# A gated hybrid decoder layer in split fp32: a sixth set of block products, block sums spread over two products, linear attention's sums on VectorE, channel tiles ahead of the branch products

## Chip, cores and metric

One core of one Trainium2 chip. The metric is the device time of one execution in microseconds (us): the median of several runs. Besides, one execution was profiled.

## What is computed

One layer (`DEPTH` = 1) on 256 tokens of 2048 channels. A normalised input goes through one wide projection; two causal mixers run in parallel (gated linear attention with 4 heads, differential attention with 16 heads); each result is gated and projected, the two are merged by sigmoid gates, projected once more and added to the input.

```python
h = rmsnorm(x, pre_norm_g)
a_q, a_k, a_v, a_g, a_lr, b_q, b_k, b_v, b_g, m_a, m_b = split(h @ w_in)
gk  = log_sigmoid(a_lr @ gla_gk_w2 + gla_gk_b) / 16
o_a = gla_chunked(a_q, a_k, a_v, gk)                # S_t = diag(exp(gk_t)) S_{t-1} + k_t^T v_t ; o_t = q_t S_t
y_a = (rmsnorm(o_a) * silu(a_g)) @ w_branch_a
o_b = diff_attention(b_q, b_k, b_v, lam)            # (softmax(q1 k1) - lam * softmax(q2 k2)) v, 128 wide per head
y_b = (rmsnorm(o_b) * (1 - lam_init) * silu(b_g)) @ w_branch_b
out = (sigmoid(m_a) * y_a + sigmoid(m_b) * y_b) @ w_out
x   = x + rmsnorm(out, post_norm_g)
```

All in fp32.

## The kernel before

**Split weights.** Every weight tile is split into a high part (a rounded copy by ScalarE, L244) and a low part (the rest, by VectorE, L245), and the activations likewise. A product is three passes on TensorE: high x high, low x high, high x low. The weights come in "halves" of 128 x 1024 elements, in the order of the list `seq` (L158 to L161). `take` (L252) hands the next half to the matmuls, and `emit_half` (L228) loads and splits up to `AHEAD` = 4 halves before it is used; high and low parts have three buffers each.

**Three ways to use a half.** `token_major` (L424) makes a 512-wide key in two banks: eight halves, twelve 128x512 matmuls each. `channel_major` (L446) makes one 128-wide channel tile (`dq`, `dk`) from two halves, with equal TensorE work per half. The third is `block_products` (L672): two 512-wide keys are made together, as a 2x2 block matrix product with seven products in place of eight (`PRODUCTS`, L28, in the order 1, 3, 5, 6, 2, 7, 4). Each product takes four halves ("half-steps") of six 128x512 matmuls. Its weight operands are blocks and sums of blocks, kept in two chains `a` and `b` (two tiles `t` of two halves `h` each): `a` is loaded, used by product 1, gets block 2 added by an accumulating DMA from the POOL queue, is used by product 5, gets `b` added on VectorE (L192) for product 6, and so on. The set's sums on VectorE are L192 (at product 6) and L199 (at product 2, with the block in `raws`). Products 1, 6, 7 and 4 add up in one PSUM bank `x`; L717 and L724 read it in between.

**Stages.** First `v0`, `v2`, `v3` directly. Then the set stage: `phase_steps` (L77) mixes the sets' half-steps with 64 "other" halves (`v4`, the linear attention's `k` and `q`, group 0's channel tiles, `m00`) by `other[len(other) * i // len(steps) : ...]` after half-step `i`. With `SETS` = 5, set 0 and 1 are merge gates and set s (s over 1) makes `dv` and `bg` (values and gates of attention group s - 2); group 3's `dv3` and `bg3` are made directly in `diff_heads(3)`. Set results are spilled to DRAM and fetched when needed. Then `ag0` to `ag3`, `m01`, attention groups 0 and 1 (`diff_heads`, L988), `m02`, the linear branch's products `y00` to `y03`, groups 2 and 3, `m03`, the attention branch's `y10` to `y13`, and the output projection `o0` to `o3`.

**Tasks.** The attention work is written as generators in a list `tasks`. `pump(step)` (L381) advances the first `step` tasks to their next `yield`; `token_major` calls it after every second half, `diff_heads` after every channel tile. Tasks in order: `forget_gate`, two `gla_scores` (one for each half of the linear heads), two `gla_out`, and for each group two `diff_pair` (two heads each; group g waits for both pairs of group g - 1). `settle` (L1059), called within `y10`, advances whatever is left until the list is empty. The order of instructions on each engine is then fixed at build time by a scheduler that starts from this order; buffers come from pools: `u` 18 tiles of 4 KB (`BIG`), `u2` 13 (`MORE`), and four PSUM banks each with the tags `mm` and `bg`. The tag `u2` holds, among others, the linear branch's operands `oah`, `oal` (four each, until `y03` is done) and the attention branch's `obh`, `obl` (one each per group, until `y13`).

**Group tiles.** For groups in `STORED` the channel tiles `dq`, `dk` are spilled and fetched by `diff_pair`; for the others `diff_split` runs at once.

Of the kernel before, what the change touches and what calls it, by code (L numbers as in the profile page):

```python
# [25 lines left out]
ROWS = {"two": 2, "tok": 4, "chan": KT}  # L26
WARM = 8
PRODUCTS = (1, 3, 5, 6, 2, 7, 4)  # L28
SETS = 5
LEAD = 6  # L30
EARLY = (0,)
STORED = (0, 1, 2)
BIG = 18
MORE = 13
BRIDGE = 512
# [56 lines left out]
def hybrid_kernel(ctx: ExitStack, tc, xt, xn, preg, postg, w, w2, gkb, glag, lamv, diffg, ident_d, causal_d, lmask_d, out):  # L92
# [57 lines left out]
    def halves_of(*keys):  # L150
        return [(key, r, h) for key in keys for r in range(len(at[key])) for h in range(2)]

    def heads_order(g):
        values = (f"dv{g}", f"bg{g}") if g + 2 >= SETS else ()
        chans = [] if g in EARLY else [f"{name}{g}{c}" for pair in range(2) for name in ("dq", "dk") for c in (2 * pair, 2 * pair + 1)]
        return halves_of(*values, *chans)

    seq = halves_of("v0", "v2", "v3") + phase_steps()  # L158
    seq += halves_of(*(f"ag{g}" for g in range(4)), "m01") + heads_order(0) + heads_order(1) + halves_of("m02")
    seq += halves_of(*(f"y0{g}" for g in range(4))) + heads_order(2) + heads_order(3) + halves_of("m03")  # L160
    seq += halves_of(*(f"{name}{g}" for name in ("y1", "o") for g in range(4)))  # L161
    ready = {}
    emitted = [0]
    raws = {}
    chain = {}

    def weights(key, r):
        a, size = at[key][r]
        return w[a : a + P * size].rearrange("(p n) -> p n", p=P), size
# [7 lines left out]
    def emit_set(s, prod, t, h):  # L177
        c = slice(1024 * h, 1024 * h + 1024)
        if h == 0 and prod == 1:
            if s == 0:  # L180
                link(s, "a", t)
            link(s, "b", t)
        if h == 0 and prod == 4 and s + 1 < SETS:
            link(s + 1, "a", t)
        n = 4 * PRODUCTS.index(prod) + 2 * t + h + LEAD - 4 * PRODUCTS.index(2)
        if 0 <= n < 4:
            i, j = n // 2, n % 2
            raws[s, i, j] = u([P, 1024], "c")
            sp.dma_start(raws[s, i, j], weights(f"set{s}", 4 + i)[0][:, 1024 * j : 1024 * j + 1024])
        a, b = chain[s, "a", t], chain[s, "b", t]  # L190
        if prod == 6:
            dve.tensor_tensor(out=a[:, c], in0=a[:, c], in1=b[:, c], op=ALU.add)  # L192
        return raws[s, t, h] if prod == 2 else (b if prod in (3, 7) else a)[:, c]

    def follow_set(s, prod, t, h):
        c = slice(1024 * h, 1024 * h + 1024)
        a, b = chain[s, "a", t], chain[s, "b", t]
        if prod == 2:
            dve.tensor_tensor(out=a[:, c], in0=a[:, c], in1=raws[s, t, h], op=ALU.add)  # L199
        if h == 1 and prod in (1, 6):  # L200
            pool.dma_start(a if prod == 1 else b, weights(f"set{s}", 2 + t)[0], accum_op=ALU.add)

    def emit_plain(j, key, r, h):
        src, size = weights(key, r)
# [47 lines left out]
    def take(key):  # L252
        j = used[0]
        used[0] += 1
        while emitted[0] < min(j + 1 + AHEAD, len(seq)):
            emit_half()
        e, hi, lo = ready.pop(j)
        assert key in (e, e[0]), (e, key)
        return hi, lo
# [118 lines left out]
    done = set()  # L378
    latest = [None]

    def pump(n=1):  # L381
        with tc.issue_after(latest[0]):
            for task in tasks[:n]:
                if next(task, DONE) is DONE:
                    tasks.remove(task)

    def product(out, pairs, first, last):
        for n, (lhs, rhs) in enumerate(pairs):
# [35 lines left out]
    def token_major(key, n, ops, step=1, settle=None):  # L424
        banks = [ps("mm"), ps("mm")]
        for q in range(KT // 2):
            if q == 6 and settle:
                settle()
            half_tile(banks, n, q, ops, *take(key))
            if q % 2 or "gate" not in done:  # L430
                pump(step)
        return banks

    def half_channel(o, h, hi, lo):
        turns = [(w, j) for w in (hi, lo) for j in range(8)]
        if h:
            turns.append(turns.pop(7))
        for w, j in turns:
            kt, c = 8 * h + j, slice(P * j, P * j + P)
            if w is hi:  # L440
                i = pe.matmul(o, hi[:, c], x_pair(kt), start=kt == 0, stop=kt == KT - 1)  # L441
            else:
                i = pe.matmul(o[:, :S], lo[:, c], x_ops(kt)[0], start=False, stop=False)  # L443
        latest[0] = i.ins

    def channel_major(key):  # L446
        o = ps("mm")
        for h in range(2):
            half_channel(o, h, *take(key))
        return o[:, :S], o[:, S:]  # L450

    def gate(bank, b, dst):
# [297 lines left out]
    def gla_scores(hf):  # L750
# [13 lines left out]
        def add_pairs(dst, src, n):  # L764
            dst = dst.rearrange("p (g t) -> p g t", t=n)
            src = src.rearrange(pairs, i=2, t=n)
            pool.tensor_tensor(out=dst, in0=src[:, :, 0, :], in1=src[:, :, 1, :], op=ALU.add)

        pool.tensor_tensor(out=suf, in0=q, in1=k, op=ALU.mult)
        add_pairs(es[:, :512], suf.rearrange("p b c t -> p (b c t)"), P)  # L770
        pool.memset(suf, 0.0)
        yield
        for n, m in enumerate(LEVELS):
# [8 lines left out]
            act.activation(xqv, view(pre, m, *late), AF.Exp, scale=1.0 / 16.0)  # L782
            dve.tensor_tensor(out=xqv, in0=xqv, in1=view(q, m, *late), op=ALU.mult)
            if m == 1:
                pool.tensor_tensor(out=xqv, in0=xqv, in1=view(k, 0, *early), op=ALU.mult)
                add_pairs(es[:, 512:], xq, 64)
                act.activation(eh, es, AF.Copy)
                dve.tensor_tensor(out=el, in0=es, in1=f32(eh), op=ALU.subtract)
                pool.memset(a, 0.0)
            else:  # L790
                act.activation(xkv, view(suf, 0, *early), AF.Exp, scale=1.0 / 16.0)
                dve.tensor_tensor(out=xkv, in0=xkv, in1=view(k, 0, *early), op=ALU.mult)
# [34 lines left out]
        act.activation(ah, aall, AF.Copy)  # L827
        dve.tensor_tensor(out=al, in0=aall, in1=f32(ah), op=ALU.subtract)
        done.add(f"scores{hf}")
        yield  # L830

    for hf in range(2):
        tasks.append(gla_scores(hf))
# [4 lines left out]
    def gla_out(hf, gates):  # L838
# [27 lines left out]
        for j in range(4):  # L866
            bank = ps("bg")
            for h in range(2):
                for b in range(2):
                    pe.transpose(bank[:, P * (2 * h + b) : P * (2 * h + b) + P], og[h][:, b, P * j : P * j + P], ident)  # L870
            i = 2 * hf + j // 2
            hi = oah[i][:, j % 2].rearrange("p h t -> p (h t)")
            lo = oal[i][:, j % 2].rearrange("p h t -> p (h t)")
            split_out(bank, hi, lo, glag_s[:, j : j + 1])
            if j % 2:
                yield
        done.add(f"out{hf}")

# [28 lines left out]
    def diff_pair(g, pair, values):  # L907
# [15 lines left out]
        for h in (2 * pair, 2 * pair + 1):  # L923
# [50 lines left out]
            dve.tensor_tensor(out=e, in0=e, in1=half_rstd, op=ALU.mult)  # L974
            for b in range(2):
                dve.scalar_tensor_tensor(out=og[:, h % 2, b, :], in0=bank[:, P * b : P * b + P], scalar=e[:, b : b + 1], in1=uu[:, b, hv], op0=ALU.mult, op1=ALU.mult)
            yield
        bank = ps("bg")
        for i in range(2):
            for b in range(2):  # L980
# [2 lines left out]
        lo = ol[:, 2 * pair : 2 * pair + 2, :].rearrange("p h t -> p (h t)")  # L983
        split_out(bank, hi, lo, diffg_s)
        done.add(f"pair{g}{pair}")
        yield

    def diff_heads(g):  # L988
        values = []
# [35 lines left out]
        return obh[kt // 4][:, kt % 4, :], obl[kt // 4][:, kt % 4, :]  # L1025

    merge_gate(token_major("m01", 512, x_ops, 2))
    diff_heads(0)
    diff_heads(1)
    merge_gate(token_major("m02", 512, x_ops, 2))  # L1030

    while not {"out0", "out1"} <= done:
        pump()
    half_done = []
    for g in range(4):
# [7 lines left out]
                act.activation(t, banks[b], AF.Copy)  # L1043
        if g < 3:
            half_done.append(spill(part, "part"))

    diff_heads(2)
    diff_heads(3)

    banks = token_major("m03", 512, x_ops, 2)  # L1050
    for b in range(2):
# [166 lines left out]
```

## Time and profile before

| | |
|---|---|
| median of 3 runs | 1121.78 us (1121.51 to 1122.82) |
| profiled execution | 1123.6 us, span from first to last instruction 1121.8 us |
| granted TensorE clock, mean | 0.997 |
| busy: PE / PEld / DVE / ACT / POOL | 1105.6 / 945.4 / 831.8 / 677.1 / 111.8 us |
| HBM read, written | 236.86 MB, 19.92 MB |

PE is TensorE's matmuls, PEld its weight loads, DVE VectorE, ACT ScalarE, POOL GpSimd, SP the queue that issues most loads. A row of a group reads: line, engine, operation, output <- inputs, shape, count, busy us, mean ns of one, and the idle time of that engine just before, with what ended most of it. A timeline row has start, duration, engine, line, and in brackets the idle time before it. A row by stage has the stretch, its length, the busy time and number of instructions of each engine, the clock, the DMA engines' share and GB/s.

### The profile page before, as it was taken

The page shows a single profiled execution, that of the slowest core. Times are in us where ns is not written, and L with a number is a line of the kernel's source. Part 1 is how long each engine was busy: PE and PEld are TensorE (multiplying, and loading weights), DVE is VectorE, ACT ScalarE, POOL GpSimd, SP SyncE. Part 2 cuts the span into 40 slices and gives each one's busy share as a digit, 9 for nine tenths or more (in the row PEclk, how much of TensorE's full clock was granted, in tenths as well). Part 3 has the DMA queues.
Part 4 walks back from the last instruction along what each step waited for, and adds up shares of the span by engine and source line. Part 5 has one row for each costly group of instructions (what it writes and reads, how often), then busy time and mean ns, then how long its engine had stood idle before and what let it go on. Part 6 is the DMA issues. An engine that isn't in the chain of part 4 may idle for free. (4 is left out here: it accounts for less than half of the span.)

```text
span 1121.8 us, 15070 instructions
## 1 busy us (share of the span) xinstructions
PE 1105.6 (99%) x5570; PEld 945.4 (84%) x5570; DVE 831.8 (74%) x1160; ACT 677.1 (60%) x997; POOL 111.8 (10%) x165
## 2 busy tenths in 40 slices
PE   9999999999999999999999999999999999999996
PEld 7998888888888888878888888788888888788886
DVE  7878979779789798699965866766676766655463
ACT  7856666666666666765655755655675665444450
POOL 0101010000100100340021202111200010000000
PEclk9999999999999999999999999999999999999998
DMA  8799797696996973945586567565645474556752
GB/s 313 261 412 243 260 321 221 221 304 188 336 254 218 313 210 123 317 167 185 174 291 243 200 220 257 202 228 176 237 165 184 158 308 161 180 188 218 269 188 75
DMA packets 46042, 257.76 MB, mean 230 GB/s; under 512 B 5841, under 2 KB 7377, under 8 KB 23441
## 3 DMA queue, kind: packets, MB, share of 16 engines
q1 hardware_dynamic: 31968, 198.59, 49.4%
q0 software_dynamic: 12992, 56.89, 18.1%
q10 hardware_dynamic: 1008, 1.32, 0.4%
q8 instruction: 43, 0.70, 0.2%
q14 instruction: 31, 0.25, 0.1%
HBM read 236.86 MB, written 19.92 MB: 229 GB/s over the span
## 5 line engine op out<-in xcount | busy, mean ns | idle before, releaser
L245 DVE TENSOR_TENSOR lo<-raw,hi 128x1024 fp32r<-128x1024 f32 (+3 forms) x307 | 369.1, 1205 | 183.8 <-ACT hi L244 180.8
L244 ACT ACTIVATE hi<-raw 128x1024 fp32r<-128x1024 f32 (+3 forms) x307 | 315.8, 1032 | 282.0 <-PE mm L421 144.6
L421 PE MATMUL mm<-hi,xs 128*128 128x512 f32 (+1 forms) x704 | 171.4, 385 | 0.0
L421 PEld LDWEIGHTS mm<-hi,xs 128*128 128x128 f32 x704 | 130.2, 188 | 21.2
L245 DVE TENSOR_TENSOR lo<-a,hi 128x1024 fp32r<-128x1024 f32 x80 | 97.2, 1221 | 19.0 <-ACT hi L244 18.0
L244 ACT ACTIVATE hi<-a 128x1024 fp32r<-128x1024 f32 x80 | 84.7, 1059 | 39.4 <-PE mm L706 20.0
L441 PE MATMUL mm<-xs,hi 128*128 128x512 f32 x384 | 100.5, 396 | 0.0
L441 PE MATMUL bg<-xs,hi 128*128 128x512 f32 x384 | 99.5, 390 | 0.2 <-ACT hi L244 0.2
L421 PE MATMUL mm<-lo,xs 128*128 128x512 f32 (+1 forms) x352 | 91.9, 383 | 0.7 <-DVE lo L245 0.7
L441 PEld LDWEIGHTS bg<-xs,hi 128*128 128x128 f32 x384 | 72.1, 188 | 14.7 <-ACT hi L244 0.6
L441 PEld LDWEIGHTS mm<-xs,hi 128*128 128x128 f32 x384 | 69.2, 189 | 11.8
L421 PEld LDWEIGHTS mm<-lo,xs 128*128 128x128 f32 x352 | 65.8, 188 | 12.9 <-DVE lo L245 1.6
L706 PE MATMUL mm<-hi,xs 128*128 128x512 f32 x240 | 65.1, 393 | 0.8 <-DVE gr L724 0.8
L443 PEld LDWEIGHTS bg<-xs,lo 128*128 128x128 f32 x384 | 52.3, 190 | 4.9 <-DVE lo L245 1.2
L443 PEld LDWEIGHTS mm<-xs,lo 128*128 128x128 f32 x384 | 52.4, 190 | 3.8
L245 DVE TENSOR_TENSOR lo<-b,hi 128x1024 fp32r<-128x1024 f32 x40 | 48.6, 1221 | 8.5 <-ACT hi L244 7.8
L443 PE MATMUL bg<-xs,lo 128*128 128x256 f32 x384 | 53.6, 282 | 0.8 <-DVE lo L245 0.8
L443 PE MATMUL mm<-xs,lo 128*128 128x256 f32 x384 | 53.5, 282 | 0.0
L706 PEld LDWEIGHTS mm<-hi,xs 128*128 128x128 f32 x240 | 44.4, 188 | 9.7 <-DVE gr L724 1.5
L421 PE MATMUL mm<-hi,oah 128*128 128x512 f32 x128 | 50.7, 396 | 0.0
L421 PE MATMUL mm<-hi,obh 128*128 128x512 f32 x128 | 50.7, 399 | 0.0
L421 PE MATMUL mm<-hi,obl 128*128 128x512 f32 x128 | 50.1, 392 | 0.0
(301 smaller groups left out, 1966.6 us busy)
## 6 DMA issues: line engine op xcount, KB each, us to landing
raw<-in_w_dram SPq DMA_DIRECT2D x136, 1024.0 KB, 5.0
raw<-in_w_dram SPq DMA_DIRECT2D x14, 832.0 KB, 6.0
a<-in_w_dram SPq DMA_DIRECT2D x10, 1024.0 KB, 6.3
b<-in_w_dram SPq DMA_DIRECT2D x10, 1024.0 KB, 7.4
c<-in_w_dram SPq DMA_DIRECT2D x20, 512.0 KB, 10.3
a<-in_w_dram POOLq DMA_DIRECT2D x10, 1024.0 KB, 15.1
b<-in_w_dram POOLq DMA_DIRECT2D x10, 1024.0 KB, 9.5
raw<-in_w_dram SPq DMA_DIRECT2D x4, 800.0 KB, 9.7
```

Source lines behind the costliest of these rows:

```text
L244: act.activation(hi_t[:, a:b], r[:, a:b], AF.Copy)
L245: dve.tensor_tensor(out=lo_t[:, a:b], in0=r[:, a:b], in1=f32(hi_t[:, a:b]), op=ALU.subtract)
L421: i = pe.matmul(banks[b][:, :n], a[part][:, P * b : P * b + P], w[:, n * j : n * j + n], start=first, stop=last)
L441: i = pe.matmul(o, hi[:, c], x_pair(kt), start=kt == 0, stop=kt == KT - 1)
L443: i = pe.matmul(o[:, :S], lo[:, c], x_ops(kt)[0], start=False, stop=False)
L706: i = pe.matmul(out, a[part], w[:, 512 * j : 512 * j + 512], start=first, stop=last, skip_group_check=out is x)
```

## The change

`SETS` becomes 6, so `dv3` and `bg3` are a sixth set, mixed with the same 64 other halves. The eight sums of a set move: `a` tile 0 gets `b` tile 0 added after the second tile of product 5, tile 1 after the first tile of product 6, and likewise for the sum at product 2 (after the second tile of 2 and the first of 7); the DMA that accumulates into `b` follows each sum of the first kind. Four elementwise operations of each `gla_scores` go from POOL to VectorE. Group 3's channel tiles are spilled and fetched too. Groups 2 and 3 are made ahead of `y00` to `y03`, with `m02` between them. `pump_eager` steps, at halves at which no `pump` is called, those of the first two tasks that stand after a pair's first head. Some `yield`s at the end of tasks go. `settle` is called after the first half of `y10`, not after the sixth.

```diff
-SETS = 5
+SETS = 6
-STORED = (0, 1, 2)
+STORED = (0, 1, 2, 3)
...
     seq = halves_of("v0", "v2", "v3") + phase_steps()
-    seq += halves_of(*(f"ag{g}" for g in range(4)), "m01") + heads_order(0) + heads_order(1) + halves_of("m02")
-    seq += halves_of(*(f"y0{g}" for g in range(4))) + heads_order(2) + heads_order(3) + halves_of("m03")
+    seq += halves_of(*(f"ag{g}" for g in range(4)), "m01") + heads_order(0) + heads_order(1) + heads_order(2)
+    seq += halves_of("m02") + heads_order(3) + halves_of(*(f"y0{g}" for g in range(4)), "m03")
...
         a, b = chain[s, "a", t], chain[s, "b", t]
-        if prod == 6:
-            dve.tensor_tensor(out=a[:, c], in0=a[:, c], in1=b[:, c], op=ALU.add)
         return raws[s, t, h] if prod == 2 else (b if prod in (3, 7) else a)[:, c]
 
     def follow_set(s, prod, t, h):
         c = slice(1024 * h, 1024 * h + 1024)
-        a, b = chain[s, "a", t], chain[s, "b", t]
-        if prod == 2:
-            dve.tensor_tensor(out=a[:, c], in0=a[:, c], in1=raws[s, t, h], op=ALU.add)
-        if h == 1 and prod in (1, 6):
-            pool.dma_start(a if prod == 1 else b, weights(f"set{s}", 2 + t)[0], accum_op=ALU.add)
+
+        def accumulate(name, i):
+            pool.dma_start(chain[s, name, i], weights(f"set{s}", 2 + i)[0], accum_op=ALU.add)
+
+        if prod == 1 and h == 1:
+            accumulate("a", t)
+        i = {(5, 1): 0, (6, 0): 1, (2, 1): 0, (7, 0): 1}.get((prod, t))
+        if i is not None:
+            a = chain[s, "a", i][:, c]
+            second = prod in (5, 6)
+            dve.tensor_tensor(out=a, in0=a, in1=chain[s, "b", i][:, c] if second else raws[s, i, h], op=ALU.add)
+            if second and h == 1:
+                accumulate("b", i)
...
+    eager = set()
+
+    def advance(some):
+        with tc.issue_after(latest[0]):
+            for task in some:
+                r = next(task, DONE)
+                (eager.add if r == "go" else eager.discard)(task)
+                if r is DONE:
+                    tasks.remove(task)
+
     def pump(n=1):
-        with tc.issue_after(latest[0]):
-            for task in tasks[:n]:
-                if next(task, DONE) is DONE:
-                    tasks.remove(task)
+        advance(tasks[:n])
+
+    def pump_eager():
+        advance([task for task in tasks[:2] if task in eager])
...
-            if q == 6 and settle:
+            if q == 1 and settle:
                 settle()
             half_tile(banks, n, q, ops, *take(key))
             if q % 2 or "gate" not in done:
                 pump(step)
+            else:
+                pump_eager()
...
             half_channel(o, h, *take(key))
+            if h == 0:
+                pump_eager()
...
-            pool.tensor_tensor(out=dst, in0=src[:, :, 0, :], in1=src[:, :, 1, :], op=ALU.add)
-
-        pool.tensor_tensor(out=suf, in0=q, in1=k, op=ALU.mult)
+            dve.tensor_tensor(out=dst, in0=src[:, :, 0, :], in1=src[:, :, 1, :], op=ALU.add)
+
+        dve.tensor_tensor(out=suf, in0=q, in1=k, op=ALU.mult)
...
-                pool.tensor_tensor(out=xqv, in0=xqv, in1=view(k, 0, *early), op=ALU.mult)
+                dve.tensor_tensor(out=xqv, in0=xqv, in1=view(k, 0, *early), op=ALU.mult)
...
         done.add(f"scores{hf}")
-        yield
...
-            if j % 2:
+            if j == 1:
                 yield
         done.add(f"out{hf}")
...
-            yield
+            yield "go" if h % 2 == 0 else None
...
         done.add(f"pair{g}{pair}")
-        yield
...
-    diff_heads(0)
-    diff_heads(1)
+    for g in range(3):
+        diff_heads(g)
     merge_gate(token_major("m02", 512, x_ops, 2))
+    diff_heads(3)
...
-
-    diff_heads(2)
-    diff_heads(3)
```

## The prediction, made before the change was run

> **What bounds the kernel now.** I read the page first, then busy time by stage, then what TensorE waited for, then the groups by line.
>
> ```profile
> PE 1105.6 (99%) x5570; PEld 945.4 (84%) x5570; DVE 831.8 (74%) x1160; ACT 677.1 (60%) x997; POOL 111.8 (10%) x165
> ...
> PEclk9999999999999999999999999999999999999998
> ```
>
> TensorE is busy for 99% of the span at the full granted clock, so the order of its instructions is the time. The other engines matter only where TensorE stands still for them. The stages (columns: PE, PEld, DVE, ACT, POOL busy, clock, DMA share, GB/s):
>
> ```profile
> 80.70:447.00 366.30, 364.38 (x1794) 309.30 (x1793) 311.70 (x311) 237.26 (x265) 29.20 (x41) 1.00 0.80 248
> 447.00:500.00 53.00, 52.45 (x236) 42.78 (x234) 39.27 (x32) 38.30 (x51) 24.67 (x24) 1.00 0.69 241
> 500.00:592.00 92.00, 91.75 (x484) 78.74 (x484) 79.09 (x109) 50.84 (x70) 5.89 (x11) 1.00 0.66 228
> ...
> 640.00:755.00 115.00, 114.09 (x561) 95.86 (x560) 76.96 (x162) 67.98 (x130) 12.88 (x23) 1.00 0.64 224
> ...
> 946.70:958.20 11.50, 10.67 (x53) 8.16 (x52) 6.89 (x22) 6.42 (x16) 0.69 (x1) 1.00 0.44 167
> ...
> PE bg L981 <- DVE ogb L976: 1.5, 2, 0.9
> PE bg L443 <- DVE lo L245: 0.8, 1, 0.8
> PE mm L706 <- DVE gr L724: 0.8, 2, 0.5
> PE mm L421 <- DVE lo L245: 0.7, 2, 0.5
> ```
>
> The first row is the stage of the block products ("set stage"), then the forget gate, the linear attention's scores, the branch products y0, and the point in y1 where the last attention tasks are flushed. TensorE stands still for 1.92, 0.55, 0.25, 0.91 and 0.83 us in them, 4.46 us in all. That is everything a better order can bring. Nearly every wait is for VectorE (DVE), which in the set stage works 311.7 of 366.3 us (85%).
>
> **Part 1: the sixth set.** The price of a 128x512 matmul comes from the chain of waits, where TensorE runs without a break:
>
> ```profile
> 972.68 16.35 PE mm L421 x72
> ```
>
> That is 0.227 us each. Direct, `dv3` and `bg3` take 2 keys x 8 halves x 12 = 192 of these matmuls. As a set they take 7 products x 4 halves x 6 = 168. So 24 go: **-5.44 us**, all on the path. What the set adds beside TensorE:
>
> ```profile
> L245 DVE TENSOR_TENSOR lo<-a,hi 128x1024 fp32r<-128x1024 f32 x80 | 97.2, 1221 | 19.0 <-ACT hi L244 18.0
> L244 ACT ACTIVATE hi<-a 128x1024 fp32r<-128x1024 f32 x80 | 84.7, 1059 | 39.4 <-PE mm L706 20.0 <-PE bg L441 10.2 <-PE mm L421 3.8
> ...
> L192 DVE TENSOR_TENSOR a<-a,b 128x1024 f32<-128x1024 f32 x20 | 24.3, 1221 | 0.2
> ...
> L684 DVE SCALAR_TENSOR_TENSOR gr<-tanh,gr 128x512 f32<-128x512 f32 x6 | 4.1, 685 | 0.0
> L724 DVE TENSOR_TENSOR gr<-mm,p 128x512 f32<-128x512 f32 x5 | 3.4, 685 | 0.0
> ```
>
> On DVE: 28 splits and 8 block sums at 1.22 us, 4 sums of products (L714, L717, L721, L724, one form) and 2 gate operations (L684) at 0.685 us, 48.0 us. TensorE gets 168 x 0.227 = 38.1 us more in this stage. DVE then has 359.7 us of work in 404.4 us: 89% in place of 85%. It stays below TensorE, with 44.7 us of slack in place of 54.6, over six sets. ScalarE's 28 x 1.06 us fit its 65% easily. The 16 direct halves leave the later stage, where DVE had room. Two tiles more are spilled and fetched (512 KB each), and the set reads 10 MB where the direct keys read 8; the stage moves 248 GB/s, its DMA share 0.80, and one set adds in proportion to its time. I cost this at nothing; if the DMA engines were the cover that is gone, it shows as the accumulate below.
>
> **Part 2: sums spread over two products.** The number and price of the sums stay (8 per set). Now all eight sit in products 6 and 2, eight half-steps in a row, in each of which DVE has 2.44 us of work against 1.36 us of TensorE. The change puts four at products 5/6 and four at 2/7, with four free half-steps between, so DVE can catch up once. Against it stands the thinner mixing: 64 other halves (2.73 us of TensorE and only 1.22 of DVE each) lie between 168 half-steps, not 140. The row of L724 shows a second spot: product 4 accumulates into the bank that L724 must read first. By the mixing formula an other half fills that spot in two of five sets now, in two of six then. Today the stage idles 1.92 us, 0.38 a set. I take 0.45 a set, 2.7 us: **+0.8**, between -1.9 (none left) and +3 (the 0.5 and 0.8 us waits above once per unfilled spot and set).
>
> **Part 3: the accumulating transfer.** In each set, `a` is read by product 1, then POOL issues a DMA that adds block 2 to it, and product 5 reads it. Issue, what ScalarE (ACT) waited, and TensorE's start (first matmul of the second half of product 5), for set 0:
>
> ```profile
> 86.08 0.89 POOL L201 DMA_DIRECT2D a<-in_w_dram  x1 [0.85 <-DVE vl L531]
> ...
> 101.69 1.06 ACT L244 ACTIVATE hi<-a 128x1024 fp32r<-128x1024 f32 x1 [2.48 <-DMA a<-in_w_dram]
> ...
> 103.35 0.40 PE L706 MATMUL mm<-hi,r1h 128*128 128x512 f32 x1
> ...
> 151.90 0.90 POOL L201 DMA_DIRECT2D a<-in_w_dram  x1
> ...
> 171.38 0.39 PE L706 MATMUL mm<-hi,r1h 128*128 128x512 f32 x1
> ...
> a<-in_w_dram POOLq DMA_DIRECT2D x10, 1024.0 KB, 15.1
> b<-in_w_dram POOLq DMA_DIRECT2D x10, 1024.0 KB, 9.5
> ...
> DMA to landing us min/median/max: 8.0/11.2/18.0
> ```
>
> In set 0 the use follows the issue by 17.3 us; the landing takes 15.1 in the median and up to 18.0, and the split must run about 1.4 us before TensorE can begin (1.06 for the high part and 1.22 for the low, which is wanted four matmuls later, 0.91). The margin is thin, and the page's shares do not show it. Seven half-steps lie between issue and use. In set 1 (last two timeline rows, first half of product 5) three other halves lie among them: 7 x 1.36 + 3 x 2.73 = 17.7 us, against 171.38 - 151.90 = 19.5 measured, so the issue leads TensorE by 1.8. Counting the formula's places, three or four other halves lie there in every set now. After the change only two do in four of the twelve transfers: 9.5 + 5.5 + 1.8 = 16.8 us, enough for a landing at 15.1, not for 18.0. I take 0.3 us for each of the four: **+1.2**, between 0 and 4 x 2.6 = 10.4 (all four at 18.0 + 1.4). The `b` accumulates are issued earlier than now (after 5/6, not 6) and need 9.5 us: nothing. [...]
>
> **Part 4: linear attention's sums on VectorE.** Per half of the heads four POOL operations move:
>
> ```profile
> 463.61 2.46 POOL L769 TENSOR_TENSOR suf<-q,k 128x1024 f32<-128x1024 f32 x1 [6.57 <-DMA k<-k]
> ...
> L767 POOL TENSOR_TENSOR att<-suf 128x512 f32<-128x512 f32 x2 | 4.0, 1980 | 0.1
> L785 POOL TENSOR_TENSOR xq<-xq,k 128x512 f32<-128x512 f32 x2 | 3.3, 1628 | 15.5 <-DVE xq L783 15.5
> ...
> 483.43 0.70 DVE L783 TENSOR_TENSOR xq<-xq,q 128x512 f32<-128x512 f32 x1 [0.21 <-ACT xq L782]
> ...
> 487.66 2.90 DVE L783 TENSOR_TENSOR xq<-xq,q 128x512 f32<-128x512 f32 x1
> 490.49 0.95 DVE L788 TENSOR_TENSOR atl<-att,ath 128x768 fp32r<-128x768 f32 x1
> 491.36 2.32 DVE L245 TENSOR_TENSOR lo<-raw,hi 128x1024 fp32r<-128x1024 f32 x1
> 493.60 1.78 DVE L794 TENSOR_TENSOR gp<-gp 128x512 f32<-128x512 f32 x1
> ...
> 498.56 0.69 DVE L794 TENSOR_TENSOR gp<-gp 128x512 f32<-128x512 f32 x1
> ```
>
> On DVE they cost 1.22 + 0.70 + 0.70 + about 0.45 (the last has 256 columns, an estimate from the 0.70 for 512) = 3.1 us, 6.2 us for both halves. But DVE gets time back: beside POOL's sums L783 took 2.90 in place of 0.70, a split 2.32 in place of 1.22, L794 1.78 in place of 0.69; these three alone are 4.4 us. So DVE's load hardly changes, and the chain through POOL into the matmuls L801 gets shorter. TensorE stands still 0.55 + 0.25 us here, mostly for splits delayed in just this place. I take half of that back: **-0.4**. One bound is -0.8. The other: the product q*k waits for the fetch of `k` (POOL waited 6.57 us for it); if it stands at that point in DVE's queue, the weight splits behind it wait too, and what the two halves of lead (5.5 us) do not cover reaches TensorE: +1 for each half of the heads, +2. [...]
>
> **Part 5: order, yields, spills.** All channel tiles now come before y0, and the attention tasks are stepped by y0 and m03. Counting steps: a group of two pairs needs ten (fetch, split, four per head less the one that the extra half-way stepping takes, twice, and the transposes); now it needs twelve. From the end of the linear attention (last channel of group 1) to the end of m03 there are 1 + 8 (channels of group 2) + 4 (m02) + 8 (group 3) + 16 (y0) + 4 (m03) = 41 steps, for 4 x 10 + 1: the last pair ends with the last step of m03. Nothing is left to flush in y1, where the 0.83 us go: **-0.8**, between -1.7 (with y0's 0.91) and 0. The four tiles of group 3 that are now spilled and fetched (256 KB each) are hidden like those of groups 1 and 2, in the row 640 to 755 DVE is at two thirds and POOL at 12.88 of 115 us. The spill of m02's gate and the fetches for y0 move past them in POOL's queue; they are needed a key later, so nothing waits.
>
> **Sum.** -5.44 + 0.8 + 1.2 - 0.4 - 0.8 = -4.6 us. The profiled execution has a span of 1121.8 us (1123.6 with what lies around it), the median of the runs is 1121.78, so the span stands for the median: **1117.2 us**. A measurement here can tell about 0.2% (2.2 us) from no change.
>
> **Rivals.**
> - *The accumulate becomes the bound* (slower). In four of twelve places TensorE waits at product 5. Break-even is where the four waits eat 1.2 + 4.6 us, 1.45 us each, a landing at 16.8 us. For it: 18.0 us is in the trace, and ACT already waited 2.48 us. Against it: the median 15.1. With all four at the longest: 1117.2 - 1.2 + 10.4 = 1126.4. DVE, with less slack afterwards, would make it worse, not better. Chance 0.18.
> - *The attention ends late* (same). The pool `u2` has 13 tiles. Before y0 ends, the linear attention's results hold 8, and the four groups' results want 8 more. Five fit: group 2's second tile and group 3's must wait until the last y0 key is past its fourth half, by my count about 33 us after the first is due, with transposed results held in two of four `bg` banks meanwhile. The step count has no slack, so a slip lands in y1. One head's chain, flushed in y1 now, from its ACT work to its transposes:
>
> ```profile
> 949.29 0.95 ACT hi L244
> ...
> 957.54 0.33 PE bg L981
> ```
>
> That is 8.3 us; today the last two halves of the y1 key cover most of it. With half of one chain open: 1117.2 + 0.8 + 4.1 = 1122.1. Chance 0.12.
> - *All idle time goes*: 1121.8 - 5.44 - 4.46 = 1111.9. For it: DVE has slack in every stage. Against it: the waits of product 4 on L724 have no cover in four sets. Chance 0.04.
> - My forecast, 1112.5 to 1119.5: chance 0.66.
>
> **How the numbers follow.** Faster by over 0.2% (below 1119.5): 0.66 + 0.04 = 0.70. Within: 0.12. Slower: 0.18. The range from 1112.0 to 1124.0 leaves out most of the first rival and the last bit of the third; forecast and second rival lie inside, 0.78, and a part of the others.
>
> **What would show it.** Right: TensorE has 24 matmuls fewer; the set stage is about 404 to 406 us long with 2 to 4 us of idle; no ACT wait for DMA `a` above 4 us; DVE's L783 near 0.70 everywhere; the last L981 before y1's second half. Wrong: TensorE waiting at L706 for `lo<-a` in several sets (first rival); L981 inside y1 with idle time around it (second); a DVE wait of some us on DMA `k` before the first scores (part 4); or a set stage in which DVE runs at 95% and more.

## The result and the profile after

The changed kernel took 1125.52 us (median of 9 runs, 1124.25 to 1127.45), the kernel before 1122.82 on the same chip (9 runs). The ratio is 1.0023, with a 95% interval of 1.0013 to 1.0033. The change made the kernel slower by 2.7 us, where 4.6 us less were forecast. The profiled execution took 1125.56 us.

The engines' busy times from the page, and then what TensorE waited for (engine and line, the releaser, total us, times, longest):

```profile
PE 1101.0 (98%) x5546; PEld 941.8 (84%) x5546; DVE 852.1 (76%) x1192; ACT 688.2 (61%) x1011; POOL 105.6 (9%) x173
...
PE mm L726 <- DVE gr L744: 2.6, 2, 2.2
PE mm L726 <- ACT hi L250: 2.0, 1, 2.0
PE bg L982 <- ACT wt L976: 1.8, 2, 1.5
...
PE bg L519 <- issue: 1.3, 1, 1.3
...
PE bg L459 <- ACT hi L250: 0.7, 1, 0.7
PE bg L437 <- ACT hi L250: 0.7, 1, 0.7
```

The 24 matmuls are gone (5570 to 5546), and TensorE is busy for 4.6 us less. Yet it stands still for 22.8 us in place of 16.2. L726, L744 and L250 are L706, L724 and L244 of before.

To see where, cut each execution in two: the set stage, and all behind it. Busy time by stretch (columns: PE, PEld, DVE, ACT, POOL, clock, DMA share, GB/s), first before, then after:

```profile
80.70:446.60 365.90, 363.98 (x1792) 308.98 (x1791) 311.37 (x311) 236.86 (x264) 29.20 (x41) 1.00 0.80 248
446.60:1121.80 675.20, 663.30 (x3378) 561.85 (x3376) 457.93 (x752) 382.60 (x633) 75.91 (x110) 1.00 0.59 208
```

```profile
80.70:492.50 411.80, 404.98 (x1960) 341.24 (x1959) 356.15 (x353) 267.60 (x298) 33.53 (x47) 1.00 0.81 248
492.50:1123.80 631.30, 618.17 (x3186) 526.40 (x3184) 433.42 (x742) 362.94 (x613) 65.27 (x112) 1.00 0.61 215
```

From the prediction's price of a matmul, the sixth set should add 168 x 0.227 = 38.1 us to the first stretch (404.0), and the sixteen direct halves should take 192 x 0.227 = 43.6 from the second (631.6). The second is 631.3. The first is 411.8, and so 7.8 us too long (the 404.0 still hold the 1.9 us for which TensorE stood still in this stage before). **The loss lies in the set stage**, in two kinds of place; a third stop lies behind it.

*The late accumulate.* Set 0: the issue on GpSimd, the split on ScalarE that reads the block, and TensorE's first matmul behind it; then the clock in the microseconds that follow:

```profile
86.01 0.88 POOL L197 DMA_DIRECT2D a<-in_w_dram  x1 [0.84 <-DVE vl L551]
...
102.13 1.06 ACT L250 ACTIVATE hi<-a 128x1024 fp32r<-128x1024 f32 x1 [5.19 <-DMA a<-in_w_dram]
...
103.23 0.50 PE L726 MATMUL mm<-hi,r1h 128*128 128x512 f32 x1 [2.00 <-ACT hi L250]
...
103.00:104.00 1.00, 0.77 (x3) 0.67 (x4) 0.79 (x1) 1.00 (x3) 0.00 (x0) 1.00 0.00 0
104.00:105.00 1.00, 0.94 (x4) 0.40 (x3) 1.00 (x2) 1.00 (x2) 0.00 (x0) 0.87 0.00 0
105.00:106.00 1.00, 1.00 (x5) 0.90 (x4) 1.00 (x2) 0.84 (x1) 0.00 (x0) 0.50 0.00 0
106.00:107.00 1.00, 1.00 (x5) 0.99 (x4) 1.00 (x2) 0.00 (x0) 0.86 (x1) 0.50 0.00 0
107.00:108.00 1.00, 1.00 (x5) 0.99 (x4) 1.00 (x2) 0.00 (x0) 0.01 (x1) 0.50 1.07 115
```

TensorE stops for 2.0 us. The sixth column (clock) then falls to 0.50 for some 3 us, and by the distance of the starts twelve matmuls lose 1.6 us more. A second stop of this kind, 0.9 us for a late low part, stands in product 5 of set 1.

*The step from product 7 to product 4.* The read of the shared bank stands behind three splits on VectorE. VectorE, then TensorE, at the end of set 0:

```profile
135.97 2.35 DVE L251 TENSOR_TENSOR lo<-a,hi 128x1024 fp32r<-128x1024 f32 x2
138.50 1.23 DVE L251 TENSOR_TENSOR lo<-a,hi 128x1024 fp32r<-128x1024 f32 x1 [0.17 <-ACT hi L250]
139.64 0.68 DVE L744 TENSOR_TENSOR gr<-mm,p 128x512 f32<-128x512 f32 x1
...
137.21 1.11 PE L461 MATMUL bg<-xs,lo 128*128 128x256 f32 x8
140.47 0.70 PE L726 MATMUL mm<-hi,xs 128*128 128x512 f32 x2 [2.15 <-DVE gr L744]
```

An other half does lie in this spot (L461 is its end), and its 2.73 us did not cover the queue. The same spot in the kernel before:

```profile
137.26 1.22 DVE L245 TENSOR_TENSOR lo<-raw,hi 128x1024 fp32r<-128x1024 f32 x1
...
138.73 1.22 DVE L245 TENSOR_TENSOR lo<-a,hi 128x1024 fp32r<-128x1024 f32 x1
...
140.20 0.68 DVE L724 TENSOR_TENSOR gr<-mm,p 128x512 f32<-128x512 f32 x1
...
140.94 1.19 PE L706 MATMUL mm<-hi,xs 128*128 128x512 f32 x4 [0.51 <-DVE gr L724]
```

Two splits stood in front of the read there, and three do now. By the distance of the starts, this step costs 2.2, 0.9, 0.45 and 0.86 us in four of the six sets, 4.4 us in all. Only the 2.2 and the 0.45 are waits for the read of the bank (sets 0 and 3). In sets 2 and 5 TensorE waits in the same spot for the high part of an other half, which ScalarE makes late (the rows of L459 and L437 above).

*The forget gate,* behind the set stage: L519 stops for 1.3 us. It is in the second stretch, where TensorE now stands still for 13.1 us in place of 11.9 (length less busy time).

### The profile page after: what moved, and what is told of

Same layout as the page of the kernel before. It is cut to its first block, busy times and chain, and to the rows that moved or that the text cites. A ratio compares the mean times of both kernels' runs of the same rounds, so it can differ in the third digit from the quotient of the medians.

```text
span 1123.8 us, 15119 instructions
## 1 busy us (share of the span) xinstructions
PE 1101.0 (98%) x5546; PEld 941.8 (84%) x5546; DVE 852.1 (76%) x1192; ACT 688.2 (61%) x1011; POOL 105.6 (9%) x173
## 4 chain that ended last, share of the span: by engine, by line
PE 85%; issue 5%; DMA 4%; ACT 2%; DVE 2%; POOL 0%; DVEq 0%; SPq 0%; POOLq 0%; ACTq 0%
PE mm L437 38%; PE mm L726 15%; PE bg L459 6%; PE mm L459 6%; DMA a<-in_w_dram 3%; PE bg L461 3%; PE mm L461 3%; PE bg L437 2%; PE bg L420 2%; PE mm L405 2%; PE mm L420 2%; DVE lo L251 1%; ACT hi L250 1%; PE bg L829 1%; PE bg L405 1%
## 5 line engine op out<-in xcount | busy, mean ns | idle before, releaser
L251 DVE TENSOR_TENSOR lo<-raw,hi 128x1024 fp32r<-128x1024 f32 (+3 forms) x291 | 345.3, 1188 | 153.9 <-ACT hi L250 144.7
L250 ACT ACTIVATE hi<-raw 128x1024 fp32r<-128x1024 f32 (+3 forms) x291 | 298.9, 1030 | 230.7 <-PE mm L437 140.1
L437 PE MATMUL mm<-hi,xs 128*128 128x512 f32 (+1 forms) x576 | 139.7, 384 | 0.0
L250 ACT ACTIVATE hi<-a 128x1024 fp32r<-128x1024 f32 x96 | 101.2, 1059 | 62.0 <-PE bg L459 19.8
L251 DVE TENSOR_TENSOR lo<-a,hi 128x1024 fp32r<-128x1024 f32 x96 | 116.4, 1220 | 26.2 <-ACT hi L250 24.8
L437 PEld LDWEIGHTS mm<-hi,xs 128*128 128x128 f32 x576 | 106.4, 188 | 16.4
L459 PE MATMUL mm<-xs,hi 128*128 128x512 f32 x384 | 101.3, 396 | 0.0
L459 PE MATMUL bg<-xs,hi 128*128 128x512 f32 x384 | 99.5, 390 | 0.7 <-ACT hi L250 0.7
L459 PEld LDWEIGHTS bg<-xs,hi 128*128 128x128 f32 x384 | 72.1, 188 | 15.3 <-ACT hi L250 1.1
L726 PE MATMUL mm<-hi,xs 128*128 128x512 f32 x288 | 77.9, 392 | 2.6 <-DVE gr L744 2.6
L459 PEld LDWEIGHTS mm<-xs,hi 128*128 128x128 f32 x384 | 69.2, 189 | 11.6
L437 PE MATMUL mm<-lo,xs 128*128 128x512 f32 (+1 forms) x288 | 74.5, 380 | 0.0
L250 ACT ACTIVATE hi<-b 128x1024 fp32r<-128x1024 f32 x48 | 50.7, 1060 | 24.1 <-PE bg L459 10.8
L726 PEld LDWEIGHTS mm<-hi,xs 128*128 128x128 f32 x288 | 53.1, 188 | 13.2 <-issue 2.3
L437 PEld LDWEIGHTS mm<-lo,xs 128*128 128x128 f32 x288 | 54.0, 188 | 9.0
L461 PEld LDWEIGHTS bg<-xs,lo 128*128 128x128 f32 x384 | 52.4, 190 | 4.1 <-DVE lo L251 0.3
L461 PEld LDWEIGHTS mm<-xs,lo 128*128 128x128 f32 x384 | 52.4, 190 | 3.8
L963 ACT ACTIVATE prob<-prob,mx,score_scale 128x128 f32<-128x128 f32 x64 | 34.3, 537 | 31.9 <-DVE mx L958 31.9
L461 PE MATMUL bg<-xs,lo 128*128 128x256 f32 x384 | 53.8, 282 | 0.0
L461 PE MATMUL mm<-xs,lo 128*128 128x256 f32 x384 | 53.5, 282 | 0.0
L437 PE MATMUL mm<-hi,oah 128*128 128x512 f32 x128 | 50.9, 397 | 0.0
```

The source lines that it names most:

```text
L250: act.activation(hi_t[:, a:b], r[:, a:b], AF.Copy)
L251: dve.tensor_tensor(out=lo_t[:, a:b], in0=r[:, a:b], in1=f32(hi_t[:, a:b]), op=ALU.subtract)
L437: i = pe.matmul(banks[b][:, :n], a[part][:, P * b : P * b + P], w[:, n * j : n * j + n], start=first, stop=last)
L726: i = pe.matmul(out, a[part], w[:, 512 * j : 512 * j + 512], start=first, stop=last, skip_group_check=out is x)
L963: act.activation(prob[m][:, lo:up], prob[m][:, lo:up], AF.Exp, scale=score_scale[:, b : b + 1], bias=mx[:, i : i + 1], accum_out=z[:, i : ...
```

## The experiments

The kernel before took 1122.82, 1122.04, 1122.77 and 1122.99 us (medians) beside the four groups of runs, each group on another chip, so kernels of different groups are compared by their ratio to it.

### The sixth set without the new order

The kernel before with `SETS = 6` and the spread sums (first kernel), and with linear attention's sums on VectorE too (second):

```diff
-SETS = 5
+SETS = 6
...
+        i = {(5, 1): 0, (6, 0): 1, (2, 1): 0, (7, 0): 1}.get((prod, t))
...
-        pool.tensor_tensor(out=suf, in0=q, in1=k, op=ALU.mult)
+        dve.tensor_tensor(out=suf, in0=q, in1=k, op=ALU.mult)
```

> The kernel before with two parts of the change alone: the sixth set and the sums spread over two products; order, yields, spills and linear attention's sums as before. Theory 1 (in the set stage the accumulating DMA into a lands too late in the places that have only two other halves in front of product 5; TensorE stands still there and in set 0 also loses its clock): the stage gives back what the 24 matmuls save, -5.4 + 4.9 us of idle + 1.9 us of low clock, about 1.4 us slower than before, 1124. Theory 2 (VectorE is short of time in the stage, wherever the other halves stand): the same here. Theory 3 (the set stage gains as forecast, the loss is in the new order of the attention): 1118 to 1119.

> As e1_sets, with linear attention's sums on VectorE too; so it is the changed kernel without the new order, yields and spills. Theory 1 and 2: 0.4 to 0.8 us under e1_sets. Theory 3: 1118. Against the changed kernel it prices the new order: theories 1 and 2 expect that to be within 1 us, theory 3 some 6 us.

Measured: 1134.69 us (ratio 1.0114, 1.0099 to 1.0130) and 1133.53 us (1.0098, 1.0085 to 1.0111). The second stretch, of the first and then of the second kernel:

```profile
492.70:1133.30 640.60, 622.80 (x3186) 526.44 (x3184) 436.75 (x734) 363.23 (x613) 77.27 (x112) 0.99 0.59 208
```

```profile
493.20:1131.30 638.10, 622.16 (x3186) 526.61 (x3184) 433.73 (x742) 364.58 (x613) 61.80 (x104) 0.99 0.59 209
```

It takes 640.6 and 638.1 us in place of 631.6. The attention tasks advance one step for every half tile or two; the direct halves of `dv3` and `bg3` carried steps, and without them tasks are left over and are flushed in y1: TensorE stands still there in seven places, six of them these waits (the same in both kernels):

```profile
PE bg L987 <- DVE ogb L982: 3.1, 3, 1.1
PE bg L961 <- DVE prob L957: 2.2, 3, 0.9
```

With the new order as well (the changed kernel) the stretch is 631.3. So, with six sets, the order is worth some 8 us, ten times its term in the prediction.

### The new order, and all but the sixth set, on five sets

The changed kernel with `SETS = 5`, old sums and old engines (the order alone), and the changed kernel with `SETS = 5` alone:

> The changed order alone (channel tiles of all heads in front of the branch products, eager steps, fewer yields, the settling at the second half of y1), with five sets, the sums of blocks in their old places and linear attention's sums on GpSimd. If the order in itself is worth what the prediction gave it, 0.8 us, and the 8 us it was worth with six sets come only from repairing what the sixth set takes away (the sixteen halves that stand in front of the attention with five sets), the time is 1120 to 1122.5 with the idle time before y1's second half gone and the attention otherwise as before. If the order is a gain of its own, the time is below 1118. If it crowds the attention so that its waits grow (the waits for wt and kl on TensorE that the changed kernel shows, 3.2 us together), the time is 1123.5 or more.

> The changed kernel with five sets: the spread sums, linear attention's sums on VectorE and the new order, without the sixth set, so that the sixth set's own worth shows beside the changed kernel. The order alone on five sets took 1129.8. If the sixth set is worth the 5.4 us of its matmuls less the stops that it brings with it in the set stage, the time is 1126 to 1130, and the changed kernel is below it. If the sixth set is what costs, and the rest a gain, the time is below 1123.

Measured: 1129.81 us (ratio 1.0065, 1.0050 to 1.0080) and 1128.57 us (1.0052, 1.0033 to 1.0071). Their second stretches:

```profile
445.50:1127.90 682.40, 665.11 (x3378) 561.91 (x3376) 455.82 (x752) 381.32 (x633) 79.17 (x118) 1.00 0.59 209
```

```profile
445.80:1126.50 680.70, 664.30 (x3378) 562.00 (x3376) 454.71 (x760) 382.58 (x633) 63.98 (x110) 1.00 0.59 210
```

The kernel before has 675.2. On five sets the order costs 7 us: with the order alone, TensorE waits in the attention for `ogb` (3.1 us in four places) and stops in some eight other places of this stretch, none longer than 1.7 us:

```profile
PE bg L994 <- DVE ogb L989: 3.1, 4, 1.3
```

So neither half stands alone: the sixth set without the order loses 12 us and the order without the sixth set 7, and together they lose 2.7. The prediction read the two as a sum of terms; they are not one.

### The spread sums and the sums on VectorE, each undone

> The changed kernel with the sums of blocks in their old places (both sums of a tile beside products 6 and 2, the accumulate behind each tile's second half of product 6). If the spread sums make the late accumulates, and these with the half clock behind them are the main loss of the set stage, the idle time of the set stage falls from 6.8 us to 3 or less and the time to 1121 to 1122.5. If the spread is a help because it takes VectorE's work away from the last products, the wait at the first product of each set for the operand that L744 writes grows, and the time is 1128 or more. If both matter little, 1125 to 1126.

> The changed kernel with linear attention's sums on GpSimd again. The prediction gave their move 0.4 us and the pair of kernels with six sets in the old order showed 1.2: with the move worth this much the time is 1126 to 1127. If the sums on VectorE are what crowds it in the scores' stage, the time is 1124 or less.

Measured: 1129.01 us (ratio 1.0054, 1.0038 to 1.0071) with the old places of the sums, 1128.66 (1.0057, 1.0042 to 1.0072) with the sums on GpSimd, against 1.0023 for the changed kernel: each is a gain of some 0.3%. The theory that the spread makes the accumulates late falls: with the old places TensorE waits for split `a` tiles and at product 4 as well. With the sums on GpSimd, VectorE's rows are stretched again:

```profile
537.08 2.90 DVE L803 TENSOR_TENSOR xq<-xq,q 128x512 f32<-128x512 f32 x1
...
540.77 2.32 DVE L251 TENSOR_TENSOR lo<-raw,hi 128x1024 fp32r<-128x1024 f32 x1
543.01 1.78 DVE L814 TENSOR_TENSOR gp<-gp 128x512 f32<-128x512 f32 x1
```

In the changed kernel no such row is left (L803 and L814 take 0.72 us at most, the splits of that stage 1.23) and TensorE doesn't stop in that stage. This trace shows two stops of 0.65 and 0.36 us there. Of the rest, 1.0 us lies in TensorE's waits at L726 in the set stage (6.3 us together, 5.3 in the changed kernel), where the sums of this part do not run. So 1 us is shown for this part, no more.

### The places of the other halves

The formula that mixes the 64 other halves in is replaced by fixed places, the same in each set. The first kernel serves the accumulates alone; the second moves the half from behind step 21 to behind step 23, in front of product 4:

```diff
+AFTER = (1, 3, 5, 7, 9, 12, 14, 17, 21, 26, 19)   # second kernel: 23 for 21
...
-        mixed += other[len(other) * i // len(steps) : len(other) * (i + 1) // len(steps)]
+        if i % 28 in AFTER[: 11 if i < 112 else 10]:
+            mixed.append(other[at])
+            at += 1
```

> The changed kernel with the 64 other halves put at fixed places: after half-steps 1, 3, 5, 7, 9, 12, 14, 17, 21, 26 (and 19 in four sets) of each set, so that four stand between every accumulate into a and its use. Nothing else differs. Theory 1: the waits at product 5 (2.2 us in set 0 with 1.9 us of low clock behind it, 1.6 in set 1, 0.4 in set 4) go, 6 us faster than the changed kernel: 1119 to 1120. Theory 2: VectorE has the same work in the same time, so within 1 us of the changed kernel: 1125.

> As e3_gap, with the other half after half-step 21 moved to after half-step 23, between product 7 and product 4, where TensorE waits for VectorE to read the bank. If those waits (2.2 us in set 0, 0.9, 0.5 and 0.9 in sets 2, 3 and 5 of the changed kernel) are due to the missing other half, 3 us under e3_gap: 1116 to 1117. If VectorE is just late there (theory 2), the same as e3_gap.

Measured: 1134.84 us (ratio 1.0112, 1.0097 to 1.0127) and 1123.50 (12 runs spread from 1118.3 to 1129.6; 1.0010, 0.9990 to 1.0029). What TensorE waited for, first and second kernel (here the bank is read in L749, and L524 is the forget gate):

```profile
PE mm L731 <- DVE gr L749: 12.0, 6, 3.4
```

```profile
PE bg L524 <- issue: 5.1, 1, 5.1
PE mm L731 <- DVE gr L749: 2.7, 2, 2.2
```

One half moved by two steps in each set is worth 11 us: the step to product 4 is the most sensitive place of the stage. In the profiled execution of the second kernel, the second longest of the twelve (1128.7), TensorE stood still at the forget gate instead.

### The late accumulates alone

One other half moved a step forward in sets 0, 1, 3 and 4, so that three lie between each accumulate and its use, nothing else changed:

```diff
...
+    moved = {10: 9, 36: 35, 94: 93, 120: 119}
+    places = [moved.get(i, i) for i in places]
```

> The changed kernel with one other half moved one step forward in each of sets 0, 1, 3 and 4, so that the four accumulates that had two other halves before their use have three, like the rest; the number of halves and every other place are as before. If the late accumulate and the half clock behind it are the loss that the prediction mis-sized, the stop at 100.9 us in set 0 (2.16 us) with the stretched matmuls behind it (1.6 us) and the 0.9 us in set 1 go: 1120.5 to 1122. If the accumulates were only the first of several late things, VectorE or the hi tiles are late next at the same places and the time is 1124 to 1126.

Measured: 1121.91 us (11 runs; ratio 0.9993, 0.9981 to 1.0005), 0.3% below the changed kernel's ratio, 3.4 us. The set stage falls to 407.7 us:

```profile
80.70:488.40 407.70, 402.82 (x1960) 340.10 (x1959) 355.57 (x353) 267.75 (x298) 33.62 (x47) 1.00 0.81 251
...
PE mm L732 <- DVE gr L750: 2.7, 2, 2.3
```

The stop of 2.0 us in front of set 0's product 5 is gone (the one wait for ScalarE's high part left at L732 is 0.5 us), and TensorE is busy for 402.8 us of the stage in place of 405.0, 2.2 less for the same matmuls, where the half clock behind that stop had cost 1.6. The step to product 4 is as in the changed kernel.

### The forget gate

One step more between the issue of the gate's four small transfers and the instructions that read them; in a second kernel, instead, the transfers on ScalarE's queue:

```diff
             pool.dma_start(w2_raw[32 * i : 32 * i + RANK, :], w2)   # second kernel: act
         yield
+        yield                                                       # first kernel
```

> The changed kernel with one more step between the issue of the forget gate's weights (four small transfers on GpSimd's queue) and the instructions that read them, so that the rest of that task runs one half tile (2.7 us) later. If the 1.46-us stop at the forget gate's matmuls comes from these transfers landing late behind the queue, the stop is gone and the time is 1123.5 to 1124.3, below the changed kernel by 1.3 to 2. If the matmuls wait for something else, or the wait is met again one task later, the time stays at 1125 to 1126.

> The changed kernel with the four small transfers of the forget gate's weights issued on ScalarE's queue instead of GpSimd's, where they stand behind the spills of the last set; the number of steps stays. If the stop of 1.46 us at the forget gate's matmuls is these transfers' place in GpSimd's queue, it goes and the time is 1123.5 to 1124.5, with the attention's stops as they are, since no step is moved (the kernel with one step more lost 8.6 us there). If the place in the queue doesn't matter, or ScalarE's own work is delayed by the issue, 1125 to 1127.

Measured: 1135.90 us (ratio 1.0123, 1.0108 to 1.0138) and 1126.70 (1.0039, 1.0024 to 1.0055). Neither removed the stop: it stayed at 1.2 us in both. With one step more the attention lost far more. In that kernel, ScalarE waits for the fetch of the next pair, and TensorE waits for the pair in hand:

```profile
811.46 1.28 ACT L918 ACTIVATE q<-dq 64x512 fp32r<-64x512 f32 x2 [5.21 <-DMA dq<-dq]
...
822.05 0.73 PE L1001 MATMUL bg<-ident,ogb 128*128 128x128 f32 x2 [6.32 <-DVE ogb L996]
...
823.00:824.00 1.00, 1.00 (x4) 0.80 (x3) 0.97 (x2) 0.97 (x2) 0.13 (x1) 0.50 1.06 451
```

The chain of waits that ends at TensorE's stop begins with that fetch: one step of shift put a waiting fetch in front of the work of a head that TensorE needed. On ScalarE's queue the transfers were issued one after the other between the operations in front, the last two at 500.8 us, and ScalarE waited 1.75 and 2.01 us for them. So in the changed kernel the queue was not the cause. In the kernel of the fixed places the same move to ScalarE's queue went with a gain, from a ratio of 1.0010 to 0.9964 (1118.81 us, next section), and with a shorter stop in the profile, 1.1 us for 5.1; there the queue may matter. The fastest kernel below does not stop there at all. What bounds these small transfers is open.

Other runs tell which part brings this stop. The sixth set in the old order has it (the line below; 0.3 us with the sums on VectorE too), and the two kernels with the new order on five sets have no such wait:

```profile
PE bg L505 <- issue: 1.5, 1, 1.5
```

So it comes with the sixth set, not with the order.

### The step to product 4 alone, and the best version

The read of the shared bank becomes a copy on ScalarE, and VectorE's addition follows in SBUF:

```diff
-                            dve.tensor_tensor(out=halves["r"][:, 1, :], in0=x, in1=kept[5], op=ALU.add)
+                            act.activation(halves["r"][:, 1, :], x, AF.Copy)
+                            dve.tensor_tensor(out=halves["r"][:, 1, :], in0=halves["r"][:, 1, :], in1=kept[5], op=ALU.add)
```

It was put on the kernel with the late accumulates mended, and on the one with fixed places and the gate's transfers on ScalarE's queue, which was run without the copy first:

> The kernel with the other halves at fixed places that serve both the accumulates and the step from product 7 to product 4, with the forget gate's weights on ScalarE's queue as well. Its profile without this showed stops of 5.1 us at the forget gate and 1.3 us of half clock behind it, and 2.2 and 1.65 at one place of set 4. If the transfers' place is the cause, the 5.1 us and the half clock go: 1117 to 1118.5, the time that the prediction gave the change. If the wide spread of its times (1118.3 to 1129.6) has another cause, the time stays between 1120 and 1125.

> The changed kernel with three other halves between every accumulate and its use (1121.9), and with the shared bank of products 6, 7 and 4 read by a copy on ScalarE behind product 7, VectorE's addition following in SBUF. If the stops at product 4's first matmul (2.4, 0.9, 0.5, 0.3 and 0.9 us in that kernel's profile, 4.9 together) come from the read's place behind three lo tiles on VectorE, most of them go: 1117.5 to 1119.5. If the bank's read is late because the matmuls in front of it end when they end, or because ScalarE has its hi tiles in front of the copy as VectorE has its lo tiles, the stops stay or move to ScalarE: 1121 to 1123.5.

> The kernel with the other halves at fixed places and the forget gate's weights on ScalarE's queue (1118.8), with the same copy on ScalarE. Its profile had 2.2 us and 1.4 us of half clock at that step in set 4 and 0.7 in set 0. If VectorE's queue is the cause: 1115 to 1116.5. If ScalarE delays the read as much: 1118 to 1121.

Measured: the fixed places with the transfers moved took 1118.81 us (ratio 0.9964, 0.9949 to 0.9978). With the copy, the first kernel took **1117.47 us** (0.9951, 0.9939 to 0.9963) and the second **1115.40 us** (0.9931, 0.9919 to 0.9944), faster than both kernels of this case. The copy in the first, and TensorE at the same step:

```profile
132.71 0.59 ACT L750 ACTIVATE gr<-mm 128x512 f32<-128x512 f32 x1
...
133.81 1.12 PE L467 MATMUL bg<-xs,lo 128*128 128x256 f32 x8
134.76 1.09 PE L732 MATMUL mm<-hi,xs 128*128 128x512 f32 x4
```

TensorE goes on without a stop; in neither kernel is the bank's read among the things that it waits for. In the first, the two waits for ScalarE's high part of an other half are still there; in the second they are not:

```profile
PE bg L465 <- ACT hi L256: 0.7, 1, 0.7
PE bg L443 <- ACT hi L256: 0.7, 1, 0.7
```

The set stage of the first, and of the second:

```profile
80.50:484.30 403.80, 401.94 (x1959) 339.93 (x1959) 355.30 (x353) 270.14 (x304) 33.48 (x47) 1.00 0.82 253
```

```profile
82.20:486.20 404.00, 403.63 (x1971) 342.39 (x1971) 357.71 (x354) 272.10 (x307) 35.12 (x49) 1.00 0.84 256
```

403.8 us is what the sixth set should take (404.0). The second row holds one other half more, 2.73 us, so 401.3 without it. VectorE still works 88% of this stage and TensorE hardly waits: its order in the queue was the trouble, not its load.

## Why the prediction was wrong, step by step

- **Part 1, the sixth set: right.** 24 matmuls are gone, and the stage with both late things mended is as long as 168 matmuls of 0.227 us make it. VectorE's load and the DMA share (0.81) came as worked out.
- **Part 2 failed in its size.** The prediction named the spot of product 4 and took 0.45 us a set for the whole stage, a term of 0.8 us, with 3 us as the bound (by waits of 0.5 and 0.8 us; the two for L724 were 0.5 and 0.3 us, 0.8 together). In the changed kernel this step costs 4.4 us in four sets, 2.65 of them behind the read of the bank. Taking VectorE out of that read gave 0.42% (0.9993 to 0.9951), 4.7 us by the medians, and 3.9 us of the set stage in the two profiles (407.7 to 403.8); the two stops on ScalarE's high part stayed. The bound was too low because it came from a trace with a shorter queue in front of L724: two splits in set 0, where three stand now. A filled spot was held to be safe; in set 0 it was filled and cost 2.2 us. By the formula two of the six spots are filled; in the trace, after the scheduler, matmuls of an other half stand there in all six sets. What stands in front of the read on VectorE has to be counted in VectorE's order.
- **Part 3 was right in its mechanism, right in one of its four places, and too small.** In the changed kernel the interval from issue to use is 16.6 to 17.2 us at exactly the four places counted, 17.7 in set 0's first tile and 18.8 or more at the others. But TensorE stopped for a late `a` in only one of the four (2.0 us in set 0), and for 0.9 us in the second tile of set 1, which the count held to be safe: 18.0 us pass there from issue to split. The price was put at 1.2 us; the runs show 3.4. In the profiled execution 1.6 us of this is the half clock behind the stop of set 0, which no row of before shows and the prediction did not think of. ScalarE's wait was to be 4 us at most and was 5.2.
- **Part 4: right,** 1 us shown in the stage for 0.4 foreseen. L803 is near 0.70 everywhere, and no wait for `k` came in its place.
- **Part 5: the sign was right and the reading was not.** The flush in y1 is gone, but on its own the order costs 7 us, and the sixth set without it costs 12. The prediction counted the steps of the changed kernel correctly and so got the sum of the two nearly right (631.3 us measured against 630.4). The stop of 1.3 us at the forget gate outweighs the 0.8; it comes with the sixth set, and part 1 has no term for it.
- **The sum.** Two terms, of product 4 and of the accumulates, were put at 2.0 us together, and mending both took the kernel from 1.0023 to 0.9951, 8.1 us. So they are about 6.1 us of the 7.3 between the forecast (4.6 faster) and the result (2.7 slower). The other 1.2 us are not traced; the stop at the forget gate is of that size, but no run removed it alone. The kernel so mended takes 1117.5 us. That this is almost the forecast of 1117.2 is luck, since the forecast held 2.0 us for the two terms that are gone in it.
- **The rivals.** "The accumulate becomes the bound" came nearest in time (1126.4), with its mechanism worth less than half of the miss (3.4 of 7.3 us); by its own break-even, 5.8 us of waits, it would not have decided alone. "The attention ends late" did not come: the last transposes of the attention are at 935 us, ahead of y1. VectorE at 86% of the stage was no bound.

The granted clock is not the same in each execution of one kernel: in the 12 runs from 1118.3 to 1129.6 us its mean is 0.996 to 0.998 in the five shortest and 0.992 to 0.994 in the seven longest. So terms below 1 us taken from one trace are uncertain.

## What to carry to other kernels

On an engine that is busy for 99% of the time, price a change by what stands in front of each releasing instruction in its own engine's queue, not by that engine's load: VectorE at 87 to 88% cost 4.7 us or nothing, depending on which engine read one bank. Where small tasks are stepped by the halves of large ones, taking halves away or adding one step moves every later meeting of the two; count the steps of both, and expect parts of such a change to have no price of their own. Add to a stop of about 2 us what the clock may take behind it: here 1.6 us behind one of 2.0, nothing behind one of 2.15.

## What the runs showed of the hardware

Behind the stop of 2.0 us in set 0 TensorE's granted clock was 0.87 between 104 and 105 us, 0.50 in the next three microseconds and 0.92 between 108 and 109, and some 1.6 us were lost by the distance of the starts. Behind another stop of about the same length in the same execution (2.15 us at product 4 of set 0) it stayed at 1.00 in each microsecond. In the kernel with one step more it was 0.50 between 823 and 824 us, behind the stop of 6.3 us that ends at 822.05. What decides whether a stop brings such a spell was not shown.
